# A decoder trunk in split fp32r: the order of fast and plain pairs in the down units, and where tiles lie in SBUF

## The chip, the cores and the metric

The kernel runs on one core of one Trainium2 chip (trn2). The metric is the device time of one execution in microseconds. The kernel before takes 2244.15 us, the median of three runs (2243.92 to 2244.21).

The engines are named as in the profile: PE is TensorE with its matmuls, PEld its weight loads, DVE is VectorE, ACT is ScalarE, POOL is GpSimd, SP is SyncE, which here only issues DMAs. A matmul multiplies a stationary operand, loaded by a weight load, with a moving operand that streams past it, and adds the product up in a bank of PSUM.

## The reference, cut to what matters

Two layers follow each other. x has 256 rows (tokens) of 2048. Each layer projects a normalised x to two groups of attention heads, maps their outputs back and adds them to x; then comes the MLP part, with 8192 hidden columns, which takes most of the time:

```
hm = rms_norm(x, mlp_norm)
up = jnp.square(jax.nn.relu(jnp.einsum('bsd,df->bsf', hm, w_up)))      # 2048 -> 8192
return x + jnp.einsum('bsf,fd->bsd', up, w_down)                       # 8192 -> 2048
```

All arrays are float32, and so is what the kernel computes.

## The kernel before

**Split operands.** A float32 product is made of three fp32r products: each operand is split in a high part and the rest, and hi*hi, hi*lo and lo*hi are added up in PSUM. For weights, ACT copies `raw` (the loaded float32 tile) to `whi` and DVE subtracts it to get `wlo`; such a pair is called the parts. Activations are split once and kept in tiles named `act`. `whi` and `wlo` have four buffers each, `raw` three; the tag `raw2` gives two more in the down units.

**Stages.** A layer runs projections and attention (`unit`, `unit_t`, L365 to L433, and the code to L898), the output projection, and then four rounds q = 0 to 3, each an up stage and a down unit. An up stage makes 2048 hidden columns in eight tiles i = 0 to 7 (`mlp_up`, L923): `unit_t` multiplies with the weight as the stationary operand, alternately 512 moving columns (`whi` against both parts of the activation, L424) and 256 (`wlo` against the high part, L428). A down unit (`mlp_down`, L961) multiplies those 2048 columns with a block of w_down of 2048 rows and adds the result to the residual `xb`. In all there are eight down units.

**The down unit.** It works in two halves of 1024 output columns (n2 = 0, 1), and in each over eight pairs j = 0 to 7 of 128-row blocks; x = 8 * n2 + j counts both, 0 to 15. A *plain* pair is computed in two steps, `left` (L1071) and `right` (L1076): eight block products, each three matmuls of 512 columns, into the banks 2 and 4 (left), 3 and 8 (right). A *fast* pair follows a Strassen-like scheme with seven block products instead of eight, in four steps with 6, 3, 6 and 6 matmuls (L1061 to L1069). DVE must form sums of weight blocks for it: the sum over two blocks (L1042) and two further adds (L1045, L1046, recorded as L1004) and one more set of parts. It also uses the banks 1, 5, 6 and 7, and on the activation side extra sums, made once in the up stage: `up_forms` (L941), four small operations on DVE (L948 to L951) and a split into a tile named `sx`. In three of its seven products the stationary operand is from `sx`, in four from `act`. Fast are j = 1, 3 and 5 (L956), so a half runs plain, fast, plain, fast, plain, fast, plain, plain.

**Drains.** After its last fast pair a half drains the banks 1, 5, 6 and 7 into `xb`: one copy on ACT (L1051) and eight operations on DVE (L1052 to L1059, recorded as L1004). After j = 7 the plain banks follow: `drain_left` adds bank 2 and bank 4, `drain_right` bank 3 and bank 8, each one DVE operation. The second half takes the same eight banks over (`new_banks`, L1006), so a first product in a bank waits for that bank's drain. Up stages and attention use the same PSUM for other tiles: `acc` (two tiles of two banks, over 5, 1 and 6, 7) and `ps` (four tiles of one bank).

**Order of the work.** PE, DVE and ACT run a down unit in the order in which it is written (`manual_schedule`, L1129). Steps pass through a queue of LEAD = 4 (L1098 to L1117): the parts of a step are prepared, and then the products of the step three places earlier are issued, with the drain that follows them. So on DVE a drain stands behind the parts of the three next steps. Around a down unit, and elsewhere, a scheduler decides the order, and it lays parts of the next stage between the last drains of a unit. Loads are issued by SP four pairs ahead.

**Places in SBUF.** The pools are laid out one after the other in the order in which they are opened (L67 to L72): constants, residual, activations, weights (with `raw`, `whi` and `wlo`), temporaries (`t2`), statistics, and behind them a scope that holds attention tiles, or `sx`, `ts`, `t4` and `raw2` in the MLP part. In bytes of each partition, by the built program: `xb` from 22,208, `act` from 38,592 to 116,416, `raw` to 140,992, `whi` and `wlo` to 173,760, `sx` from 185,152 to 194,368, `raw2` to 210,752.

Of the kernel before, what the change touches and what calls it, by code (L numbers as in the profile page):

```python
# [10 lines left out]
F32R = mybir.dt.float32r  # L11
# [5 lines left out]
P = 128  # L17
# [22 lines left out]
def trunk_kernel(  # L40
# [22 lines left out]
    def nm(s):  # L63
        uid[0] += 1
        return f"{s}_{uid[0]}"

    cpool = ctx.enter_context(tc.tile_pool(name="const", bufs=1))  # L67
    xpool = ctx.enter_context(tc.tile_pool(name="resid", bufs=1))
    apool = ctx.enter_context(tc.tile_pool(name="acts", bufs=19))
    wpool = ctx.enter_context(tc.tile_pool(name="weights", bufs=3))  # L70
    tpool = ctx.enter_context(tc.tile_pool(name="temps", bufs=2))
    spool = ctx.enter_context(tc.tile_pool(name="stats", bufs=6))  # L72

    pools = {}
    scopes = {}
# [28 lines left out]
    def tmp(tag, shape, dt=F32, bufs=2):  # L104
        pool = pools["att"] if tag in ATT else pools["mlp"] if tag in MLP else tpool
        return pool.tile(list(shape), dt, tag=tag, name=nm(tag), bufs=bufs)
# [13 lines left out]
    def f32(ap):  # L120
        return ap.bitcast(F32)
# [218 lines left out]
    def weight_parts(w2d, r0, c0, kt, width, fine=False, halves=1, order=lambda k: None):  # L340

        full = 2048 // kt
        raw = wpool.tile([P, kt, full], F32, tag="raw", name=nm("raw"))
        src = w2d[r0 : r0 + kt * P, c0 : c0 + width].rearrange("(k p) n -> p k n", p=P)
        step = 1 if fine else kt // halves
        for s in range(0, kt, step):
            nc.sync.dma_start(raw[:, s : s + step, :width], src[:, s : s + step, :])
        for s in range(2):
            hk = kt // 2
            hi = wpool.tile([P, hk, full], F32R, tag="whi", name=nm("whi"), bufs=4)  # L350
            lo = wpool.tile([P, hk, full], F32R, tag="wlo", name=nm("wlo"), bufs=4)
            step = 1 if fine else hk
            for q in range(0, hk, step):
                r = raw[:, s * hk + q : s * hk + q + step, :width]
                h = hi[:, q : q + step, :width]
                dep = order(s * hk + q)
                with tc.issue_after(dep) if dep else nullcontext():
                    newest["hi"] = nc.scalar.activation(h, r, AF.Copy).ins  # L358
                with tc.issue_after(st["first"]) if fine else nullcontext():
                    newest["lo"] = nc.vector.tensor_tensor(  # L360
                        lo[:, q : q + step, :width], r, f32(h), ALU.subtract
                    ).ins
            yield hi, lo
# [240 lines left out]
    for l in range(DEPTH):  # L604
# [348 lines left out]
            split(op.pair(i), t)  # L953

        def fast(i):
            return i in (1, 3, 5)  # L956

        hT = Operand()
        ssq2 = new_ssq()
# [1 line left out]
        def mlp_down(q):  # L961
# [23 lines left out]
                )  # L985

            def parts(r, n=2):
                hi = wpool.tile([P, 2, 512], F32R, tag="whi", name=nm("whi"), bufs=4)
                lo = wpool.tile([P, 2, 512], F32R, tag="wlo", name=nm("wlo"), bufs=4)
                nc.scalar.activation(hi[:, :n], r, AF.Copy)  # L990
                nc.vector.tensor_tensor(lo[:, :n], r, f32(hi[:, :n]), ALU.subtract)  # L991
                return hi, lo

            def mm(m, a, w, c, last):

                (ah, al), (wh, wl) = a, w
                o = banks[m]
                nc.tensor.matmul(o, ah, wh[:, c], start=m not in begun, stop=False)
                begun.add(m)
                nc.tensor.matmul(o, ah, wl[:, c], start=False, stop=False)  # L1000
                nc.tensor.matmul(o, al, wh[:, c], start=False, stop=last)

            def add(dst, a, b, sub=False):
                nc.vector.tensor_tensor(dst, a, b, ALU.subtract if sub else ALU.add)  # L1004
# [6 lines left out]
            def steps(x):  # L1011

                n2, j = pairs[x]
                last = j == 7
                r = raws[x]
                d = op.t[j]
                x11, x21, x12, x22 = (xb[2 * n2 + c][:, tt, :] for c in range(2) for tt in range(2))

                def blk(k, tt):
                    sl = slice(tt * P, (tt + 1) * P)  # L1020
                    return d[:, k, 0, sl], d[:, k, 1, sl]

                def ext(i):
                    return op.x[j][:, i, 0, :], op.x[j][:, i, 1, :]

                def store(c, tt):
                    if end:
                        n = 2 * n2 + c
                        nc.sync.dma_start(
                            ov[:, tt, n * 512 : (n + 1) * 512], xb[n][:, tt, :]  # L1030
                        )

                if fast(j):
                    sums = {}
                    lastf = j == 5

                    def first():
                        t13 = sums["t13"] = tmp("ts", [P, 2, 512], bufs=2)
                        t4 = sums["t4"] = tmp("t4", [P, 512], bufs=1)
                        b12 = r[:, 0, 512:]  # L1040
                        ends = r.rearrange("p k (c n) -> p (k c) n", c=2)[:, ::3, :]
                        nc.vector.tensor_tensor(  # L1042
                            t13, ends, b12.unsqueeze(1).to_broadcast([P, 2, 512]), ALU.add
                        )
                        add(b12, t13[:, 0, :], r[:, 1, 512:])  # L1045
                        add(t4, b12, r[:, 1, :512])  # L1046
                        return parts(r[:, 1, :].rearrange("p (c n) -> p c n", c=2))

                    def drain():
                        dw = tmp("t2", [P, 512], bufs=4)  # L1050
                        nc.scalar.activation(dw, banks[1], AF.Copy)  # L1051
                        add(x12, banks[5], x12)  # L1052
                        add(x22, banks[5], x22)
                        add(x11, banks[1], x11)
                        add(dw, banks[6], dw, True)
                        add(x12, dw, x12)
                        add(dw, banks[7], dw)
                        add(x21, x21, dw, True)
                        add(x22, dw, x22)  # L1059

                    return (  # L1061
                        (first, lambda w: (mm(2, blk(1, 0), w, 0, False), mm(3, ext(1), w, 1, False)), None),
                        (lambda: parts(sums["t4"].unsqueeze(1), 1), lambda w: mm(4, blk(1, 1), w, 0, False), None),
                        (lambda: parts(sums["t13"]),
                         lambda w: (mm(5, blk(0, 1), w, 0, lastf), mm(7, ext(2), w, 1, lastf)), None),
                        (lambda: parts(r[:, 0, :].rearrange("p (c n) -> p c n", c=2)),
                         lambda w: (mm(1, blk(0, 0), w, 0, lastf), mm(6, ext(0), w, 1, lastf)),
                         drain if lastf else None),
                    )  # L1069

                def left(w):  # L1071
                    for m, tt in ((2, 0), (4, 1)):
                        for k in range(2):
                            mm(m, blk(k, tt), w, k, last and k == 1)

                def right(w):  # L1076
                    for m, tt in ((3, 0), (8, 1)):
                        for k in range(2):
                            mm(m, blk(k, tt), w, k, last and k == 1)

                def drain_left():
                    add(x11, banks[2], x11)
                    store(0, 0)
                    add(x21, banks[4], x21)
                    store(0, 1)

                def drain_right():
                    add(x12, banks[3], x12)
                    store(1, 0)
                    add(x22, banks[8], x22)  # L1090
                    store(1, 1)

                return (
                    (lambda: parts(r[:, :, :512]), left, drain_left if last else None),
                    (lambda: parts(r[:, :, 512:]), right, drain_right if last else None),
                )
# [13 lines left out]
            for x in range(len(pairs)):  # L1110
                load(x + 4)
                for prepare, products, follow in steps(x):
                    queue.append((x, products, prepare(), follow))
                    if len(queue) >= LEAD:
                        emit(*queue.pop(0))
# [55 lines left out]
```

## Time and profile before

| | |
|---|---|
| median of three runs | 2244.15 us |
| the profiled execution | 2244.34 us |
| its span, first to last instruction | 2242.6 us |
| instructions in the span | 28,461 |
| granted TensorE clock, mean | 1.000 |
| mean DMA rate over the span | 182 GB/s |
| HBM read | 405.12 MB |

The span is 1.7 us shorter than the execution around it. Rows of a timeline give the start in microseconds from the span's start, the time taken, engine, line, operation, and output and input tiles by the program's names; "x3" is a run of three merged rows, and the bracket behind a row is the idle time before it with what ended it. A line can be that of a helper: all adds of the down unit have L1004. Rows of groups give the count, the busy time, the mean of one in ns, and the idle time just before.

### The profile page before, as it was taken

The page shows a single profiled execution, that of the slowest core. Times are in us where ns is not written, and L with a number is a line of the kernel's source. Part 1 is how long each engine was busy: PE and PEld are TensorE (multiplying, and loading weights), DVE is VectorE, ACT ScalarE, POOL GpSimd, SP SyncE. Part 2 cuts the span into 40 slices and gives each one's busy share as a digit, 9 for nine tenths or more (in the row PEclk, how much of TensorE's full clock was granted, in tenths as well). Part 3 has the DMA queues.
Part 4 walks back from the last instruction along what each step waited for, and adds up shares of the span by engine and source line. Part 5 has one row for each costly group of instructions (what it writes and reads, how often), then busy time and mean ns, then how long its engine had stood idle before and what let it go on. Part 6 is the DMA issues. An engine that isn't in the chain of part 4 may idle for free.

```text
span 2242.6 us, 28461 instructions
## 1 busy us (share of the span) xinstructions
PE 2219.7 (99%) x11292; PEld 1858.6 (83%) x11292; DVE 1628.6 (73%) x2024; ACT 1171.0 (52%) x1499; POOL 39.1 (2%) x68
## 2 busy tenths in 40 slices
PE   9999999999999999999999999999999999999998
PEld 7988778887888888788788887888878878887887
DVE  5777565668868868867967775656787688688688
ACT  5555354555555455455555553555555545554553
POOL 0020000000000000000000200000000000000000
PEclk9999999999999999999999999999999999999999
DMA  6545446664665665565446544466656656656653
GB/s 228 189 158 162 151 144 232 187 188 169 214 186 188 201 188 187 190 195 179 169 135 204 171 151 150 154 225 184 188 183 203 187 178 207 188 181 210 185 180 127
DMA packets 250857, 409.05 MB, mean 182 GB/s; under 512 B 6650, under 2 KB 162882, under 8 KB 250724
## 3 DMA queue, kind: packets, MB, share of 16 engines
q1 hardware_dynamic: 250724, 407.24, 55.7%
q8 instruction: 88, 1.44, 0.3%
q14 instruction: 45, 0.37, 0.0%
HBM read 405.12 MB, written 2.10 MB: 182 GB/s over the span
## 4 chain that ended last, share of the span: by engine, by line
PE 91%; DVE 7%; issue 1%; ACT 1%; DMA 0%; POOL 0%; SPq 0%; POOLq 0%
PE acc L424 24%; PE acc L428 12%; PE acc L377 9%; PE acc L378 9%; PE acc L379 9%; DVE wlo L991 3%; DVE xb L1004 2%; DVE t L1004 1%; PE ps L294 1%; PE ps L847 1%; PE ps L859 1%; DVE ts L1042 0%; PE ps L806 0%; ACT whi L990 0%; PE ps L540 0%
## 5 line engine op out<-in xcount | busy, mean ns | idle before, releaser
L360 DVE TENSOR_TENSOR wlo<-raw,whi 128x1024 fp32r<-128x1024 f32 (+2 forms) x530 | 630.5, 1194 | 420.0 <-ACT whi L358 418.9
L358 ACT ACTIVATE whi<-raw 128x1024 fp32r<-128x1024 f32 (+2 forms) x530 | 545.3, 1032 | 643.9 <-PE acc L424 340.0
L424 PE MATMUL acc<-act,whi 128*128 128x512 f32 x2304 | 816.0, 399 | 0.0
L428 PE MATMUL acc<-act,wlo 128*128 128x256 f32 x2304 | 646.8, 281 | 0.0
L424 PEld LDWEIGHTS acc<-act,whi 128*128 128x128 f32 x2304 | 433.0, 188 | 106.5
L428 PEld LDWEIGHTS acc<-act,wlo 128*128 128x128 f32 x2304 | 435.2, 189 | 0.4
L377 PE MATMUL acc<-whi,act 128*128 128x512 f32 (+2 forms) x960 | 368.4, 384 | 0.5 <-ACT act L302 0.5
L378 PE MATMUL acc<-wlo,act 128*128 128x512 f32 (+2 forms) x960 | 361.9, 377 | 0.4 <-DVE wlo L360 0.4
L379 PE MATMUL acc<-whi,act 128*128 128x512 f32 (+2 forms) x960 | 361.6, 377 | 0.0
L991 DVE TENSOR_TENSOR wlo<-raw,whi 128x1024 fp32r<-128x1024 f32 x256 | 306.2, 1222 | 70.0 <-ACT whi L990 65.6
L990 ACT ACTIVATE whi<-raw 128x1024 fp32r<-128x1024 f32 x256 | 266.2, 1058 | 157.3 <-PE acc L424 29.0
L377 PEld LDWEIGHTS acc<-whi,act 128*128 128x128 f32 x960 | 180.9, 188 | 35.5 <-issue 4.1
L379 PEld LDWEIGHTS acc<-whi,act 128*128 128x128 f32 x960 | 180.5, 188 | 33.8 <-issue 0.7
L378 PEld LDWEIGHTS acc<-wlo,act 128*128 128x128 f32 x960 | 180.8, 188 | 32.0 <-DVE wlo L360 1.0
L990 ACT ACTIVATE whi<-t 128x512 fp32r<-128x512 f32 x48 | 30.4, 634 | 145.5 <-DVE t L1004 93.3
L991 DVE TENSOR_TENSOR wlo<-ts,whi 128x1024 fp32r<-128x1024 f32 x48 | 58.8, 1225 | 2.3 <-ACT whi L990 2.3
L1042 DVE TENSOR_TENSOR ts<-raw 128x1024 f32<-128x1024 f32 x48 | 58.5, 1218 | 0.0
L939 DVE TENSOR_TENSOR act<-t,act 128x512 fp32r<-128x512 f32 x64 | 44.1, 690 | 10.9 <-ACT act L938 10.9
L990 ACT ACTIVATE whi<-ts 128x1024 fp32r<-128x1024 f32 x48 | 50.2, 1045 | 0.0
L439 DVE TENSOR_TENSOR t<-acc,t 128x512 f32<-128x512 f32 x72 | 49.3, 684 | 0.0
L934 ACT ACTIVATE t<-t 128x512 f32<-128x512 f32 x64 | 39.6, 618 | 12.8 <-DVE t L930 12.8
L930 DVE SCALAR_TENSOR_TENSOR t<-t,row 128x512 f32<-128x512 f32 x64 | 44.3, 692 | 2.2
(1160 smaller groups left out, 2768.2 us busy)
## 6 DMA issues: line engine op xcount, KB each, us to landing
raw<-in_w_down_dram SPq DMA_DIRECT2D x128, 1024.0 KB, 5.3
raw<-in_w_up_dram SPq DMA_DIRECT2D x128, 1024.0 KB, 5.8
raw<-in_w_in_dram SPq DMA_DIRECT2D x84, 1024.0 KB, 5.1
raw<-in_w_o_dram SPq DMA_DIRECT2D x32, 1024.0 KB, 5.0
raw<-in_w_in_dram SPq DMA_DIRECT2D x14, 512.0 KB, 6.8
raw<-in_w_in_dram SPq DMA_DIRECT2D x8, 544.0 KB, 3.7
out_dram<-xb SPq DMA_DIRECT2D x8, 256.0 KB, 2.2
xb<-in_x_dram SPq DMA_DIRECT2D x3, 512.0 KB, 7.5
```

The lines of the kernel that those rows point to most:

```text
L358: newest["hi"] = nc.scalar.activation(h, r, AF.Copy).ins
L360: newest["lo"] = nc.vector.tensor_tensor(lo[:, q : q + step, :width], r, f32(h), ALU.subtract).ins
L377: nc.tensor.matmul(o, xh[:, sl], whi[:, j, :width], start=first, stop=False)
L378: nc.tensor.matmul(o, xh[:, sl], wlo[:, j, :width], start=False, stop=False)
L379: st["mm"] = nc.tensor.matmul(o, xl[:, sl], whi[:, j, :width], start=False, stop=last).ins
L424: nc.tensor.matmul(acc[:, f, :], whi[:, j, sl], op.both(k), start=(k == 0), stop=False, skip_group_check=True,)
L428: nc.tensor.matmul(acc[:, f, T:], wlo[:, j, sl], xh, start=False, stop=(k == KT - 1), skip_group_check=True,)
L439: nc.vector.tensor_tensor(t, acc[:, :, :T], t, ALU.add)
L990: nc.scalar.activation(hi[:, :n], r, AF.Copy)
L991: nc.vector.tensor_tensor(lo[:, :n], r, f32(hi[:, :n]), ALU.subtract)
L1004: nc.vector.tensor_tensor(dst, a, b, ALU.subtract if sub else ALU.add)
L1042: nc.vector.tensor_tensor(t13, ends, b12.unsqueeze(1).to_broadcast([P, 2, 512]), ALU.add)
```

## The change

Two things change. Fast are now j = 2, 4 and 6, so that a half runs plain, plain, fast, plain, fast, plain, fast, plain, and with it the flag of the last fast pair goes from 5 to 6. And the pools lie elsewhere: `whi` and `wlo` get a pool of their own, `parts`; `act`, `parts` and the scope stay at the lower side of SBUF, and constants, residual, `raw`, temporaries and statistics are put at its upper side. By the built program, `act` then lies from 16,512 to 94,336, `whi` and `wlo` to 127,104, `sx` from 127,104 to 136,320, `raw2` to 152,704; `raw` from 182,688 to 207,264, `xb` to 223,648, and the constants above.

```diff
-    cpool = ctx.enter_context(tc.tile_pool(name="const", bufs=1))
-    xpool = ctx.enter_context(tc.tile_pool(name="resid", bufs=1))
+    cpool = ctx.enter_context(tc.tile_pool(name="const", bufs=1, side="right"))
+    xpool = ctx.enter_context(tc.tile_pool(name="resid", bufs=1, side="right"))
     apool = ctx.enter_context(tc.tile_pool(name="acts", bufs=19))
-    wpool = ctx.enter_context(tc.tile_pool(name="weights", bufs=3))
-    tpool = ctx.enter_context(tc.tile_pool(name="temps", bufs=2))
-    spool = ctx.enter_context(tc.tile_pool(name="stats", bufs=6))
+    ppool = ctx.enter_context(tc.tile_pool(name="parts", bufs=4))
+    wpool = ctx.enter_context(tc.tile_pool(name="weights", bufs=3, side="right"))
+    tpool = ctx.enter_context(tc.tile_pool(name="temps", bufs=2, side="right"))
+    spool = ctx.enter_context(tc.tile_pool(name="stats", bufs=6, side="right"))
...
-            hi = wpool.tile([P, hk, full], F32R, tag="whi", name=nm("whi"), bufs=4)
-            lo = wpool.tile([P, hk, full], F32R, tag="wlo", name=nm("wlo"), bufs=4)
+            hi = ppool.tile([P, hk, full], F32R, tag="whi", name=nm("whi"), bufs=4)
+            lo = ppool.tile([P, hk, full], F32R, tag="wlo", name=nm("wlo"), bufs=4)
...
         def fast(i):
-            return i in (1, 3, 5)
+            return i in (2, 4, 6)
...
             def parts(r, n=2):
-                hi = wpool.tile([P, 2, 512], F32R, tag="whi", name=nm("whi"), bufs=4)
-                lo = wpool.tile([P, 2, 512], F32R, tag="wlo", name=nm("wlo"), bufs=4)
+                hi = ppool.tile([P, 2, 512], F32R, tag="whi", name=nm("whi"), bufs=4)
+                lo = ppool.tile([P, 2, 512], F32R, tag="wlo", name=nm("wlo"), bufs=4)
...
                 if fast(j):
                     sums = {}
-                    lastf = j == 5
+                    lastf = j == 6
```

## The prediction

> **What bounds the kernel now.** I read the page first (busy shares, costly groups), then the waits of PE, then timelines of one down unit, and last the spacing of the matmuls.
>
> ```profile
> span 2242.6 us, 28461 instructions
> PE 2219.7 (99%) x11292; PEld 1858.6 (83%) x11292; DVE 1628.6 (73%) x2024; ACT 1171.0 (52%) x1499; POOL 39.1 (2%) x68
> L424 PE MATMUL acc<-act,whi 128*128 128x512 f32 x2304 | 816.0, 399 | 0.0
> L428 PE MATMUL acc<-act,wlo 128*128 128x256 f32 x2304 | 646.8, 281 | 0.0
> L377 PE MATMUL acc<-whi,act 128*128 128x512 f32 x832 | 331.1, 398 | 0.5 <-ACT act L302 0.5
> ...
> PE m__862_4746 L998 <- DVE xb L1004: 1.8, 1, 1.8
> ...
> PE m__3241_18213 L998 <- DVE xb L1004: 1.8, 1, 1.8
> ```
>
> PE is busy 99% of the span, so only two things can move the time: how long PE waits, and how far apart its matmuls start. A matmul's own duration (399 ns) overlaps the next, so I count starts. Its waits are few: the first and the last of eight equal ones of 1.8 us are shown, one in the middle of each down unit, where the second half of the columns takes over the PSUM banks. One more that matters, at L294 where layer 1 begins, stands in a row below.
>
> **The middle of a down unit.** I call the two halves of a plain pair L and R and the four steps of a fast pair a to d; 8L is step L of x = 8.
>
> ```profile
> 2007.32 0.40 PE L998 MATMUL m__2925_16452<-whi,act 128*128 128x512 f32 x1
> 2008.55 1.28 DVE L1004 TENSOR_TENSOR xb<-m__2921_16448,xb 128x512 f32<-128x512 f32 x2
> ...
> 2013.72 3.49 DVE L991 TENSOR_TENSOR wlo<-raw,whi 128x1024 fp32r<-128x1024 f32 x3
> 2017.13 0.68 DVE L1004 TENSOR_TENSOR xb<-m__2925_16452,xb 128x512 f32<-128x512 f32 x1
> 2018.33 1.21 DVE L1042 TENSOR_TENSOR ts<-raw 128x1024 f32<-128x1024 f32 x1
> 2020.73 0.39 PE L1001 MATMUL m__2993_16777<-whi,act 128*128 128x512 f32 x1
> 2022.05 0.68 DVE L1004 TENSOR_TENSOR xb<-m__2927_16454,xb 128x512 f32<-128x512 f32 x1
> 2022.88 0.47 PE L998 MATMUL m__2994_16778<-whi,act 128*128 128x512 f32 x1 [1.76 <-DVE xb L1004]
> ```
>
> At 2007.32 the last fast pair (x = 5) is done and PE starts 6L. DVE drains the fast banks in eight operations, 2008.55 to 2013.72. PE has four plain halves in hand (6L to 7R, 10.91 us) and reaches 8L at 2018.23, when the adds of banks 2 and 4 have started (2017.13 and 0.60 later), so it goes on. 8L ends at 2020.73 + 0.23 = 2020.96. 8R writes bank 3, whose add starts only at 2022.05: the fast pair x = 9 stands ahead of it in DVE's order (L1042 at 2018.33 and three more). PE restarts 0.83 us after that add starts. The wait is 22.88 - 20.96 = 1.92 us.
>
> **The change, part one: fast pairs at 2, 4, 6.** The work is the same: as many products, DVE, ACT and DMA instructions. In the middle the plain pair x = 9 now follows x = 8, so the operations that held up bank 3 go behind it. But the last fast pair is now x = 6, and only 7L and 7R lie between it and 8L. DVE's order there is, by the built program: eight drains, parts of 8R, adds of banks 2 and 4, parts of 9L, adds of 3 and 8, parts of 9R, then x = 10. I lay it on the clock above, with 7L starting at 2007.32, since x = 6 stands behind a plain pair as x = 5 did:
> - PE ends 7R at 2007.32 + 24 x 0.2267 = 2012.76 and wants bank 2.
> - DVE ends the drains at 2013.72, parts of 8R take 1.14 (3.49 for three, overlapping), bank 2's add starts at 2014.86, PE restarts 0.83 later: 2015.69. What is late next is this add: a wait of 2.93 us.
> - The bank 3 add follows after 0.60 + 0.60 + 1.14: 2017.20, ready 2018.03, and 8L ends at 2015.69 + 2.72 = 2018.41. The old wait is gone.
> - Parts of 10a are ready at about 2023.3; PE needs them at 2018.41 + 3 x 2.72 = 2026.6. Covered by 3.3 us.
>
> So 1.92 becomes 2.93: **+1.0 us, eight times, +8.1**. It holds if DVE ends the parts before the drain when it does now; half a microsecond either way gives +4 to +12.
>
> At the end of a unit the eight drains now lie beside 15L and 15R alone. DVE starts them one step earlier (parts of 14R are no longer ahead): 2051.36 in the clock of the rows below, where 14L starts at 2051.27 and so 15L would; PE is free at 2051.27 + 5.44 = 2056.71.
>
> ```profile
> 2040.92 0.40 PE L998 MATMUL m__2992_16776<-whi,act 128*128 128x512 f32 x1
> ...
> 2047.74 4.83 DVE L991 TENSOR_TENSOR wlo<-raw,whi 128x1024 fp32r<-128x1024 f32 x4 [1.10 <-ACT whi L990]
> 2051.27 0.40 PE L998 MATMUL m__2992_16776<-whi,act 128*128 128x512 f32 x1
> ...
> 1123.19 0.39 PE L1001 MATMUL m__1604_9040<-whi,act 128*128 128x512 f32 x1
> 1124.37 0.69 DVE L1004 TENSOR_TENSOR xb<-m__1604_9040,xb 128x512 f32<-128x512 f32 x1
> 1125.11 0.77 PE L294 MATMUL ps<-ident,xb 128*128 128x128 f32 x5 [1.09 <-DVE xb L1004]
> ...
> 2238.29 0.39 PE L1001 MATMUL m__3242_18214<-whi,act 128*128 128x512 f32 x1
> 2238.71 0.69 DVE L1004 TENSOR_TENSOR xb<-m__3242_18214,xb 128x512 f32<-128x512 f32 x1 [0.67 <-PE m__3242_18214 L1001]
> ```
>
> - Six borders to an up unit: the next accumulator needs banks 5 and 1, drained by about 2053.3, and its parts, which stand between the drains: ready 2054.9, before 2056.71. Cost 0; this cover is 1.8 us.
> - The border of the layers needs the four plain banks for its transposes. Four drains of 0.60, three parts of 1.14 and seven adds of 0.60 stand before bank 8's add: it starts at 2061.4 and is ready 0.74 later, 5.4 us after PE is free, against 1125.11 - 1123.42 = 1.69 now: **+3.8** (0 to 4.4).
> - At the end of the kernel no parts lie between: bank 8's add starts at 2051.36 + 5.17 + 3 x 0.60 = 2058.3, 1.6 us after PE's end, against 0.19 now (2238.71 - 2238.52): **+1.4** (0.5 to 1.5).
>
> The start of a unit gains nothing: no wait of PE stands there to be removed. The forms of fast pairs (L948 to L951 and their split) move one up tile later; an up tile takes PE 32 x 0.353 = 11.3 us, and DVE four parts of 1.14 and under 4 us of smaller operations, so PE hides them; uncovered, they are five operations of at most 0.60 us, 3 us for each of 24. Loads keep their order; on SP only the last load and two stores of the last unit change places.
>
> **Part two: addresses.** By the built programs act moves from 38 to 116 thousand bytes of each partition down to 17 to 94, whi and wlo from 141 to 174 down to 94 to 127, sx from 185 to 194 down to 127 to 136; raw, xb, temps and constants go up. No instruction changes. What an operand's place costs is not shown directly; the spacing of starts bounds it.
>
> ```profile
> 84.19 0.39 PE L377 MATMUL acc<-whi,act 128*128 128x512 f32 x1
> ...
> 86.46 0.39 PE L378 MATMUL acc<-wlo,act 128*128 128x512 f32 x1
> ...
> 78.73 0.28 PE L379 MATMUL acc<-whi,act 128*128 128x256 f32 x1
> ...
> 80.64 0.28 PE L377 MATMUL acc<-whi,act 128*128 128x256 f32 x1
> ...
> 2128.95 0.40 PE L424 MATMUL acc<-act,whi 128*128 128x512 f32 x1
> ...
> 2130.01 0.40 PE L424 MATMUL acc<-act,whi 128*128 128x512 f32 x1
> ```
>
> With a low act as the stationary, 512 columns take 2.27/10 = 0.227 us and 256 take 1.91/16 = 0.119 to 0.120. From x = 12 to x = 14 (2040.92 to 2051.27) 45 matmuls take 10.35, where 45 x 0.2267 = 10.20: the fast pair between pays 0.147 us, 16 ns for each of its nine matmuls with sx, the highest stationary; over 48 fast pairs **7.1 us**. sx differs from act in nothing but its place, and lies 58 thousand bytes lower afterwards, so I take all of it back; the ends are 0 and 7.1. A pair in an up unit takes 1.06/3 = 0.3533, where 0.2267 + 0.120 = 0.3467. That 6.7 ns may be the place of whi and wlo or the alternating width; I leave it in place, since the width differs as well, and price it as a rival.
>
> The Trainium skill speaks against this part: SBUF — State Buffer, section "Who interferes with whom", gives TensorE two read ports of its own and says that "PE and ACT never wait on anyone". By that rule the place of an operand is worth nothing and the third term is 0; it is rival 1.
>
> **The sum.** The profiled execution took 2244.34 us (span 2242.6 and 1.7 around it), 0.2 over the median of 2244.15. 2244.3 + 8.1 + 3.8 + 1.4 - 7.1 = **2250.5**; with the bounds, 2242 to 2262.
>
> **Rivals.**
> 1. The addresses do nothing. For it: plain matmuls start 0.227 apart however busy ACT and DVE are. Against it: the 16 ns of sx. 2257.6.
> 2. Faster after all: the pairs of the up units fall from 0.3533 to 0.3467 because whi and wlo lie low. 2304 x 6.7 ns = 15.4 us, so 2235.1. For it: sx, also a high stationary, is slow too. Against it: widths 512 and 256 alternate only there. It decides from 2.7 ns a pair, (13.3 - 7.1)/2304.
> 3. Both operands low is a state that no fp32r matmul here has been in, and part of the fixed cost goes. From 0.2267 and 0.120 a column costs 0.417 ns, so 512 cost 213.4 and 13.3 ns are fixed; 33 ns in a pair. At most (3 x 832 + 8 x 366, the matmuls of a down unit) x 13.3 + 2304 x 33 = 148 us: 2244.3 + 13.3 - 148 = 2110 (the loss of sx would be gone with it). Against it: nothing but the place of either operand would have to cause it. The Trainium skill's TensorE: Matmul & The Clock Gate, section "Wait — 56ns, not 53.3ns?", gives columns / 2.4 GHz + 2.5 ns, 215.7 for 512; the trace has 227.
> 4. Two operands in the same part of SBUF hinder each other, as sx and whi, both high, would now. Then low beside low costs 10 ns in each of 10,416 matmuls (2 x 2304 in up units, 2880 plain ones and 2928 of down units): 2244.3 + 13.3 + 104 = 2362.
>
> **How the numbers follow.** Forecast 0.30, rival 1 0.20, rival 2 0.29, rival 3 0.10, rival 4 0.06, a smaller schedule cost than I counted 0.05. The range 2233 to 2262 takes in the forecast's bounds and rivals 1 and 2, and leaves out 3 and 4. A measurement tells 0.2%, 4.5 us, from no change: faster is below 2239.7 (most of rival 2, 0.26, and rival 3: 0.36), slower above 2248.6 (0.23 of the forecast, rivals 1 and 4, 0.01: 0.50), the rest 0.14.
>
> **What would show it.** Right: eight waits of PE, now before the first L998 of bank 2 in the second half, 2.7 us each by the wait view; none before bank 3; a wait near 5 us at L294; sx steps of 0.227. The pair of the up units tells rival 2 (0.347) from the forecast (0.353), and the step of 512 columns tells 3 (0.215) and 4 (0.237). Wrong would be a middle wait under 1.5 us: DVE then reaches bank 2 sooner than I lay out.

## The result and the profile after

The changed kernel takes 2268.28 us (median of four runs, 2268.14 to 2271.2), against 2244.18 us (2243.92 to 2244.59) before: a ratio of 1.011, 95% interval 1.0093 to 1.0128. The forecast was 2250.5 us, the range 2233 to 2262, so the direction was right and the size was not: +24 us where +6 had been worked out. The profiled execution took 2268.14 us, its span is 2266.4 us.

From the page of the changed kernel, then its wait view for PE (total, times, longest in us), then the view of cores. Lines of the kernel are one higher than before, since a pool was added: L999 is the old L998.

```profile
span 2266.4 us, 28474 instructions
PE 2229.6 (98%) x11292; PEld 1870.6 (83%) x11292; DVE 1625.9 (72%) x2024; ACT 1171.7 (52%) x1499; POOL 39.1 (2%) x68
L425 PE MATMUL acc<-act,whi 128*128 128x512 f32 x2304 | 816.3, 399 | 0.0
L429 PE MATMUL acc<-act,wlo 128*128 128x256 f32 x2304 | 646.9, 281 | 0.0
```
```profile
PE ps L295 <- DVE xb L1005: 4.6, 2, 3.5
PE m__2743_15343 L999 <- DVE xb L1005: 2.9, 1, 2.9
...
PE m__2496_13912 L999 <- DVE xb L1005: 2.8, 1, 2.8
```
```profile
core 0: 2266.4 us, clock 0.992
```

The eight middle waits are longer, as forecast: 2.8 to 2.9 us in this view against 1.8, and they now stand ahead of bank 2. The waits at L295 grew too, from 1.1 us to 4.6 in all. But the waits explain only about half of the 24 us. What nobody had priced is in the last line: a mean granted TensorE clock of 0.992, where it was 1.000 before. A share of 0.8% of the span sounds like little; it is the cause of the miss.

The DVE timeline of the last middle wait (start, time taken) shows the wait as it was laid out: eight drains, the parts of 8R, and only then the add of bank 2.

```profile
2210.15 1.28 DVE L1005 TENSOR_TENSOR xb<-m__3166_17877,xb 128x512 f32<-128x512 f32 x2
...
2214.72 0.68 DVE L1005 TENSOR_TENSOR xb<-t,xb 128x512 f32<-128x512 f32 x1
2215.32 1.22 DVE L992 TENSOR_TENSOR wlo<-raw,whi 128x1024 fp32r<-128x1024 f32 x1
2216.46 0.68 DVE L1005 TENSOR_TENSOR xb<-m__3170_17881,xb 128x512 f32<-128x512 f32 x1
```

The PE timeline of the same place:

```profile
2214.06 0.39 PE L1002 MATMUL m__3173_17884<-whi,act 128*128 128x512 f32 x1
2217.29 0.47 PE L999 MATMUL m__3237_18209<-whi,act 128*128 128x512 f32 x1 [2.84 <-DVE xb L1005]
...
2218.43 0.63 PE L1001 MATMUL m__3237_18209<-wlo,act 128*128 128x512 f32 x1
2218.85 0.63 PE L1002 MATMUL m__3237_18209<-whi,act 128*128 128x512 f32 x1
...
2220.99 0.63 PE L1001 MATMUL m__3238_18210<-wlo,act 128*128 128x512 f32 x1
2221.41 0.45 PE L1002 MATMUL m__3238_18210<-whi,act 128*128 128x512 f32 x1
2221.70 0.40 PE L999 MATMUL m__3239_18211<-whi,act 128*128 128x512 f32 x1
```

7R's last matmul starts at 2214.06 and its step ends at 2214.29; 8L starts at 2217.29, after a wait of 3.00 us. Then, 0.8 us after the restart, the starts fall to 0.427 us apart (2218.43 to 2220.99 is 2.56 for six steps), twice the usual 0.227, and come back at 2221.5. No engine is waited for there. The same place in four windows of 3.41 us, with PE's busy time and matmuls, the granted clock (PEclk), the busy share of the DMA engines and GB/s:

```profile
2211.29:2214.70 3.41, 3.16 (x14) 1.00 0.72 292
2214.70:2218.12 3.42, 0.83 (x4) 1.00 0.16 24
2218.12:2221.53 3.41, 3.41 (x10) 0.50 0.86 237
2221.53:2224.94 3.41, 3.41 (x17) 1.00 1.03 374
```

The window in which PE was busy for only 0.83 us is followed by one at half clock, although PE is busy all through that one. The records of the granted clock show the same after seven of the eight middle waits, for two windows after one of them, and for two at the border of the layers: ten such windows of 3.413 us within the span, and their starts lie on one grid of 3.413 us. Before, there is none within the kernel's matmuls.

For the whole account I take every start-to-start step of PE, less 0.4167 ns a column and 13.3 ns (the line through 226.7 ns for 512 columns and 120 for 256), and sort the remainder (us, before and after): middle waits 15.4 and 24.1; border of the layers 1.3 and 5.4; behind the last start 4.3 and 6.2; steps in down units outside half clock 8.2 and 0.8; **steps at half clock 0 and 14.4**; up units 16.6 and 16.9; other waits 4.6 and 5.6; the rest 50.6 and 51.5. The changes add up to the 23.8 us between the two spans. Where a wait reaches into a half-clock window its class is a choice, which moves about 1 us between the border, the half clock and the other waits.

### The profile page after: what moved, and what is told of

The parts are those of the page before. It is cut to its first block, busy times and chain, and to the rows that moved or that the text cites. A ratio compares the mean times of both kernels' runs of the same rounds, so it can differ in the third digit from the quotient of the medians.

```text
span 2266.4 us, 28474 instructions
## 1 busy us (share of the span) xinstructions
PE 2229.6 (98%) x11292; PEld 1870.6 (83%) x11292; DVE 1625.9 (72%) x2024; ACT 1171.7 (52%) x1499; POOL 39.1 (2%) x68
## 4 chain that ended last, share of the span: by engine, by line
PE 93%; DVE 4%; issue 1%; ACT 1%; DMA 0%; POOL 0%; SPq 0%; DVEq 0%; POOLq 0%
PE acc L425 24%; PE acc L429 12%; PE acc L378 9%; PE acc L379 9%; PE acc L380 9%; DVE xb L1005 2%; DVE wlo L992 1%; PE ps L295 1%; DVE t L1005 1%; PE ps L848 1%; PE ps L860 1%; ACT whi L991 0%; PE ps L807 0%; PE ps L541 0%; PE ps L487 0%
```

## The experiments

My theory after the result: the middle wait of 3.0 us leaves PE idle through most of one 3.413 us window, and the half clock that follows costs as much again as the longer waits; the places gain their 7 us, which is hidden below it. Rivals: the half clock comes from the new places; or it has nothing to do with idle time. The kernel before took medians of 2244.43 to 2244.95 us beside these runs.

**The order alone** (old places, fast pairs at 2, 4, 6).

```diff
-            return i in (1, 3, 5)
+            return i in (2, 4, 6)
...
-                    lastf = j == 5
+                    lastf = j == 6
```

> Fast pairs at 2, 4, 6 with the old places in SBUF. Theory (the longer wait in the middle drops the TensorE clock to half for a while): the same waits of 3.0 us and the same half-clock stretches as in the changed kernel, and the loss of 147 ns in each of 48 fast pairs is back: 2268.2 + 7.1 = 2275.3 us, granted clock near 0.992. Rival (the half clock comes from the new places): the clock stays at 1.000, and only the schedule's 14 us are lost: about 2258 us.

Measured 2264.66 us (2263.14 to 2267.72), ratio 1.0094 (1.0079 to 1.0109). That is below what my theory gave and above the rival. The trace has the middle waits, 2.90 us each, and half clock without the new places, so the rival falls. But it has only three windows of half clock, not ten, two in the middle of units and one at the border of the layers: in the six other middles the wait lay across the border of two windows of the grid, as 1.39 and 1.50 us for example, and no half clock followed. The size of the miss is the number of windows hit, 4.4 us of half clock here against 14.4. I had carried the count of the changed kernel over to another one, whose waits of nearly the same length lie otherwise on the grid.

**The places alone** (new places, fast pairs at 1, 3, 5; the opposite edit, on the changed kernel).

> New places in SBUF with the fast pairs left at 1, 3, 5. Theory: the fast pairs gain their 147 ns, the waits stay at 1.92 us, the clock stays at 1.000: 2244.2 - 7.1 = 2237.1 us. Rival (the half clock comes from the new places): the clock falls below 0.995 here too and the time is 2250 us or more.

Measured 2246.87 us, ratio 1.0011 (1.0003 to 1.002), but spread from 2242.74 to 2250.66 over eleven runs, with a granted clock between 0.998 and 0.995. By the letter the expectation missed. In its trace the steps of the fast pairs are right (1.4 us left of 8.2), and the middle waits are 2.02 us, not 1.92: the fast pair ahead of each wait is 0.1 us quicker and DVE is not, so PE arrives sooner and waits longer (with the loss of sx put back, below, the wait is 1.93 us again). And 2.02 us can be enough for half clock, where they fall within one window: four of the eight waits were followed by it in the profiled execution. The windows at one of them:

```profile
1666.64:1670.05 3.41, 3.41 (x17) 1.00 1.00 382
1670.05:1673.47 3.42, 1.55 (x8) 1.00 0.43 164
1673.47:1676.88 3.41, 3.41 (x10) 0.50 0.00 0
1676.88:1680.29 3.41, 3.41 (x16) 1.00 0.15 19
```

So the kernel before stood 0.1 us below waits that can cost half clock, and the gain in the fast pairs alone carries it there.

**The wait filled** (the changed kernel with twelve matmuls ahead of 8L, whose products are thrown away).

```diff
                     new_banks()
+                    if x == 8:
+                        for _ in range(12):
+                            nc.tensor.matmul(
+                                banks[5], op.t[0][:, 0, 0, :P], w[0][:, 0],
+                                start=True, stop=True,
+                            )
                 products(w)
```

> The changed kernel with twelve matmuls of 512 columns, whose product is thrown away, put ahead of the first product of the second half, into a bank that is drained by then. The wait for bank 2 ends when it did, but PE is idle for 0.3 us of it and not 3.0. Theory: no half clock in the middle of a unit, about 13.5 us less: 2254.7 us; only the border of the layers still has one. Rival (the half clock has nothing to do with the idle time of PE, or what follows a wait is slow for another reason): unchanged at 2268 us, or more.

Measured 2254.11 us (2253.32 to 2255.77), ratio 1.0043 (1.003 to 1.0057): the theory. It does more work than the changed kernel, DVE's order is the same, and it is 14 us faster. Its clock and its only large waits of PE for DVE:

```profile
core 0: 2252.7 us, clock 0.998
```
```profile
PE ps L295 <- DVE xb L1005: 4.4, 2, 3.5
```

The border of the layers was not filled and kept its two windows of half clock; no other is left within the kernel's matmuls.

**One matmul against the cliff** (the places alone, with a single such matmul ahead of 8R).

> New places, fast pairs at 1, 3, 5, and one matmul of 512 columns, whose product is thrown away, ahead of 8R: the middle wait of 2.02 us ends as before, but PE is idle for 1.80 us of it. Theory (over about 2.0 us idle within one window of 3.41 us halves the clock): no half clock in any run, where the kernel without the filler has up to four or more: 2238.4 us and little spread, against 2242.7 to 2250.7. Rival (the half clock has another cause, or the limit lies lower): as without the filler, around 2247 us.

Measured 2238.54 us (2238.34 to 2239.82, eight runs), ratio 0.9972 (0.9961 to 0.9983): the theory to 0.2 us, and the spread of 8 us is gone. The place in its PE timeline, with the added matmul first, and its clock:

```profile
2191.64 0.39 PE L1106 MATMUL m__3235_18217<-whi,act 128*128 128x512 f32 x1
2193.57 0.50 PE L999 MATMUL m__3241_18223<-whi,act 128*128 128x512 f32 x1 [1.54 <-DVE xb L1005]
2193.90 0.40 PE L1001 MATMUL m__3241_18223<-wlo,act 128*128 128x512 f32 x1
2194.14 0.39 PE L1002 MATMUL m__3241_18223<-whi,act 128*128 128x512 f32 x1
```
```profile
core 0: 2236.6 us, clock 1.000
```

PE is idle for 1.70 us instead of 2.02; 0.23 of the difference is the added matmul, and the restart comes 0.09 us sooner, which no run explains. This is also the price of the places without half clock: 6.3 us below the kernel before (2244.85 beside it). In its trace the steps of the down units give 6.6 us, and the middle, with the added matmuls counted in, costs what it did before (15.4 us in all).

**A longer wait** (the places alone, with one more DVE add, result thrown away, ahead of bank 3's).

> New places, fast pairs at 1, 3, 5, and one more DVE operation of 0.69 us, whose result is thrown away, ahead of the add of bank 3 in the first half: the middle wait becomes 2.6 us instead of 1.92. Theory (the clock is judged in windows of 3.41 us, and one with more than about 2 us idle halves it): half clock after some of the eight waits, four or five, by how they lie to the windows: 2237.1 + 5.5 + 5 x 1.7 = 2251 us. Rival (only a wait of 3 us or more halves it): none, 2242.6 us.

Measured 2253.22 us in one run: near the theory's 2251, and well above the rival's 2242.6. The wait became 2.82 us, 0.2 more than I had put (1.8 us in all, under either view), and five of the eight were followed by half clock; it is these five, and not the time alone, that rule the rival out. The three that were not lay across a border of the grid, with at most 2.04 us in one window.

**Which place matters.** sx alone put high, then whi and wlo alone put high, then sx moved up by 10 thousand bytes, all with fast pairs at 1, 3, 5.

```diff
-        open_scope("sbuf", mlp=1)
+        open_scope("sbuf", mlp=1, sx=1)
...
-                    **({"space": PSUM} if space == "psum" else {}),
+                    **({"space": PSUM} if space == "psum" else {"side": "right"} if key == "sx" else {}),
```

> New places with fast pairs at 1, 3, 5, but sx put high (162 to 171 thousand bytes), act, whi and wlo staying low. Theory (a high stationary tile costs by itself): the irregular steps of 228 to 241 ns behind each product with sx are back, 147 ns a fast pair. Rival (the two operands hinder each other where both lie high): none, since whi and wlo are low; steps of 227 ns.

Measured 2244.04 us, clock 1.000: the theory. Its PE timeline at a fast pair, and that of the changed kernel:

```profile
1982.23 0.40 PE L999 MATMUL m__2929_16464<-whi,sx 128*128 128x512 f32 x1
...
1989.16 0.39 PE L999 MATMUL m__2929_16464<-whi,act 128*128 128x512 f32 x1
```
```profile
2004.97 0.39 PE L999 MATMUL m__2925_16452<-whi,sx 128*128 128x512 f32 x1
...
2008.37 0.39 PE L999 MATMUL m__2921_16448<-whi,sx 128*128 128x512 f32 x1
```

With sx high, 30 steps take 6.93 us where 30 x 0.2267 are 6.80; with sx low, 15 steps take 3.40, as plain ones do. The moving operand was low in both, so sx as a high stationary tile costs by itself. With the loss the middle wait is back at 1.93 us, and no window is at half clock.

```diff
-    ppool = ctx.enter_context(tc.tile_pool(name="parts", bufs=4))
+    ppool = ctx.enter_context(tc.tile_pool(name="parts", bufs=4, side="right"))
```

> New places with fast pairs at 1, 3, 5, but whi and wlo put high (174 to 207 thousand bytes), act and sx staying low. Theory (a stationary tile that lies high, as sx did, costs its matmuls 47 ns a product, whatever the moving operand's place): every matmul step of a fast pair takes 227 ns, as with whi and wlo low. Rival (moving and stationary operand hinder each other where both lie high): also 227 ns, since only one is high now; the next kernel separates the two. A third view (high whi and wlo cost by themselves): steps above 227 ns throughout the down units.

Measured 2258.01 us, clock 1.000: what I had listed only as a third view. In its PE timeline 12 steps take 2.80 us, 0.2333 each, in plain and fast products alike:

```profile
2049.83 0.40 PE L999 MATMUL m__2992_16779<-whi,act 128*128 128x512 f32 x1
...
2052.63 0.40 PE L999 MATMUL m__2991_16778<-whi,sx 128*128 128x512 f32 x1
```

So a moving operand at 174 to 207 thousand bytes costs too, 6.7 ns a matmul, while at 141 to 174 (before) the plain step was 226.7 ns, as at 94 to 127. In the up units, where whi and wlo are the stationary operand, the mean pair fell from 353.8 to 350.0 ns. Height is therefore not simply bad; what sets the sign is open.

> New places with fast pairs at 1, 3, 5, and sx at 137 to 147 thousand bytes: 10 thousand above the changed kernel's place, where it cost nothing, and 25 thousand below the place where it cost its full price. Theory (a limit by height): either the steps behind sx stay at 227 ns and the limit lies above 147, or they are irregular and it lies near 137 thousand. Rival (the distance to act counts, no limit): something between, under 147 ns a fast pair.

Measured 2249.8 us, with seven windows of half clock behind waits of 2.02 us. The steps behind sx are 226.7 ns. So the distance to act doesn't count, and if a limit by height is what counts, it lies for sx between 147 and 162 thousand bytes. (The pools were split by `open_scope("sbuf", mlp=1, sx=1, raw2=1)`.)

**The drain in two** (the changed kernel, the five later adds of the fast drain postponed behind the add of bank 8 in the first half). In the last unit the first half's blocks are stored ahead of these adds, so that part of the output lacks them.

```diff
+                        def rest():
+                            add(dw, b6, dw, True)
...
+                        if n2 == 0:
+                            later.append(rest)
+                        else:
+                            rest()
```

> The changed kernel with the drain of the fast banks in the first half cut in two: the three adds of banks 5 and 1 stay where they are, the five others follow the add of bank 8, so that the adds of banks 2 and 4 no longer stand behind them. Theory: the middle wait of 3.0 us is gone, and the half clock with it: 2244.2 - 7.1 - 15.4 + 3.7 + 1.9 and some 3 of half clock at the border of the layers: 2230 us. Rival (DVE has too much to do there in any order): a wait of 1 to 3 us turns up later in the unit, at the first steps of x = 10, 2238 to 2255 us.

Measured 2232.91 us (2231.98 to 2233.26), ratio 0.9946 (0.993 to 0.9963): the theory within 3 us. No middle wait is left. One new wait of 3.2 us lies in the last unit alone, with a window of half clock behind it:

```profile
2185.33 0.69 DVE L1006 TENSOR_TENSOR xb<-t,xb 128x512 f32<-128x512 f32 x1 [4.68 <-DMA out_dram<-xb]
...
2189.27 0.79 PE L1002 MATMUL m__3239_18211<-wlo,act 128*128 128x512 f32 x1 [3.07 <-DVE wlo L993]
```

There the postponed adds have to await the stores of the first half: DVE stands for 4.68 us, and the parts that PE needs are late by it.

**The drain ahead of the fast pair** (the places alone; 7R and the drain of banks 3 and 8 issued before the fast pair x = 9 is prepared).

```diff
                 for prepare, products, follow in steps(x):
+                    if x == 9 and queue[0][0] == 7:
+                        emit(*queue.pop(0))
                     queue.append((x, products, prepare(), follow))
```

> New places, fast pairs at 1, 3, 5, and in the middle of a unit the products of 7R and the drain of banks 3 and 8 are issued before the parts of the fast pair x = 9 rather than behind its first step. Theory: the middle wait of 2.02 us is gone, and so is the half clock it sets off at times: 2244.2 - 7.1 - 15.4 = 2221.8 us. Rival (the fast pair is then late): PE waits for its first step instead, up to 1 us in each of eight places: up to 2230 us.

Measured 2219.12 us (2218.97 to 2220.18), ratio 0.9885 (0.987 to 0.99). DVE's timeline in the middle:

```profile
1998.42 0.68 DVE L1005 TENSOR_TENSOR xb<-m__2927_16457,xb 128x512 f32<-128x512 f32 x1
1999.01 0.68 DVE L1005 TENSOR_TENSOR xb<-m__2928_16458,xb 128x512 f32<-128x512 f32 x1
1999.61 1.22 DVE L1043 TENSOR_TENSOR ts<-raw 128x1024 f32<-128x1024 f32 x1
```

Bank 3's add (m__2927) now runs ahead of the fast pair's first operation, the middle wait is gone, the pair is not late, and the clock is 1.000. It is 2.7 us better than worked out. The mean pair of the up units fell from 353.8 to 352.6 ns, 2.8 us in all, and it did so in the drain in two as well; why, no run shows.

**Widths in twos** (on top of that: in the up units two matmuls of 512 columns, then two of 256, in place of taking turns).

```diff
                             start=(k == 0), stop=False, skip_group_check=True,
                         )
+                    for f in range(2):
+                        sl = slice(f * P, (f + 1) * P)
                         nc.tensor.matmul(
```

> The kernel of e8 (new places, fast pairs at 1, 3, 5, drain ahead of the fast pair) with the products of an up unit in another order: two of 512 columns and then two of 256, instead of 512 and 256 by turns. Theory A (the alternating width costs the 6.7 ns of a pair): the mean of a pair falls from 0.352 us by 3 to 7 ns, 8 to 15 us of 2219 us less: about 2207 us. Theory B (the place or the kind of the stationary tile costs it): unchanged, 2219 us.

Measured 2210.82 us (2210.41 to 2211.99), ratio 0.9849 (0.9835 to 0.9864): 8.3 us better than without. Its PE timeline merges two matmuls of a kind in a row:

```profile
2094.70 0.63 PE L425 MATMUL acc<-act,whi 128*128 128x512 f32 x2
...
2097.49 0.63 PE L425 MATMUL acc<-act,whi 128*128 128x512 f32 x2
```

Eight pairs take 2.79 us, 0.349 each; over all 2304 the mean is 349.1 ns against 352.6. So the order of the up unit's matmuls makes about half of the excess that rival 2 had put down to the place of whi and wlo. The edit also puts two stationary tiles of `whi` and then two of `wlo` in a row, where they took turns; the width and the order of the tiles were not tried apart. This is the fastest kernel of the study, 1.5% below the one before.

## Why the prediction was wrong

- **The middle of a unit.** Right in place, cause and nearly in length: 2.93 us forecast, 3.00 measured, 2.90 with the old places. The 0.1 us between is the gain of the fast pair ahead, given back in the wait; the sum counted that gain in full. Term +8.1, measured +8.7.
- **The borders.** +3.8 forecast for the border of the layers (its own figures, 5.4 less 1.69, give 3.7), +4.1 measured in the account. Read as the forecast reads it, PE is free at 1131.55 + 0.23 = 1131.78 and restarts behind bank 8 at 1137.24, 5.46 us later:

```profile
1131.55 0.39 PE L1002 MATMUL m__1602_9038<-whi,act 128*128 128x512 f32 x1
1135.44 0.66 PE L295 MATMUL ps<-ident,xb 128*128 128x128 f32 x4 [3.51 <-DVE xb L1005]
1137.24 2.82 PE L295 MATMUL ps<-ident,xb 128*128 128x128 f32 x12 [1.14 <-DVE xb L1005]
```

For the end +1.4 was forecast and +1.9 measured. Up units wait for nothing, as said.
- **Part two, sx.** -7.1 forecast, -7.4 measured in the steps of the down units. The place was the cause, as the run with sx high showed; rival 1 falls.
- **Rival 2 falls.** The pairs of the up units are unchanged, 353.8 and 353.9 ns, though whi and wlo moved; put high, they made the pair faster, 350.0. Rivals 3 and 4 fall with the plain step, 0.2267 before and after.
- **The step that failed** is the use made of "only two things can move the time: how long PE waits, and how far apart its matmuls start". The sum treats the two as independent: it prices each longer wait at its own length (+8.1, +3.8) and puts what a wait does to the starts behind it at nothing. The runs showed that those starts depend on it: past about 2 us idle in one window the clock halves for at least 3.41 us, and a step takes 0.427 us instead of 0.227. That put 14.4 us on top, more than any term that was counted, and it was not among the rivals; all other changes add up to 9.4 us, against the 6.2 forecast. With the middle waits filled the time fell by 14 us. The profile's clock of 1.000 before was read as a given, not as the state of a kernel whose waits end just short of the limit.

The Trainium skill has the mechanism, in TensorE: Matmul & The Clock Gate, section "What's actually happening": a free-running window of 3413 ns, and half clock after at least one idle window. The window agrees with the grid of 3.413 us here. The dose does not: a wait of 2.02 us, with PE busy for the other 1.4 us of the window, was enough in four of eight places. Read by that section's letter, the waits of 3.0 us would have stayed at full clock.

## What to carry to other kernels

A wait of the bounding engine can have a price beyond its length: on this kernel 1.9 us of idle TensorE were paid once, and from about 2.0 us within one window on up to 1.6 us came on top. When a change lengthens a wait, or only speeds up the work ahead of it, compare the new wait with that limit and look at the granted clock by windows of 3.41 us, not at its mean. The best remedy here was to remove the wait, by moving the drain ahead of the fast pair; where a wait stayed, one to twelve matmuls into a free bank kept the clock.

## What the runs showed of the hardware

- **The limits of the clock.** I laid every idle time of PE in thirteen traces (from a start plus its step to the next start) on the 3.413 us grid that each trace's own half-clock records give. Counting idle stretches of over 0.2 us, 183 windows at full clock have over 0.3 us idle: none with up to 1.91 us was followed by half clock, all 18 with 2.22 us or more were, and between 1.92 and 2.04 us 12 of 25 were; what decides there is open. Of the half-clock windows with over 0.3 us idle, the five with up to 0.59 us were followed by full clock, the four with 0.68 or more by another half.
- **Where in SBUF an operand lies** changes the step of its matmul, with the same instructions on every engine: about 50 ns for each product of three matmuls with sx as the stationary tile at 162 to 171 or 185 to 194 thousand bytes (6.8 and 7.4 us over 144 products), nothing at 127 to 147; 6.7 ns for each matmul with the moving operand at 174 to 207, nothing at 94 to 127 or 141 to 174. It is no rule for every stationary tile: whi and wlo, stationary in the up units, were 3.8 ns a pair faster at 174 to 207. The Trainium skill's rule that PE never waits on anyone (SBUF — State Buffer, "Who interferes with whom") does not cover this: a place has a price here, and whether PE waits for anyone in these steps the traces don't show.
- **Order in the up unit.** Taking turns between 512 columns of `whi` and 256 of `wlo` costs about 3.5 ns a pair against twos of each.
